# A decoder step's state-space scan: the masked step sums as two products over high and low parts

## The chip, the cores and the metric

The kernel runs on one core of one Trainium2 chip. The metric is the device time of one execution in microseconds. A core has a matrix engine (PE, with its weight loads shown apart as PEld), a vector engine (DVE), a scalar engine (ACT), a general engine (POOL) and queues for transfers, most of them issued by SP. Each engine works through its own row of instructions in order and waits on semaphores for the others.

## The reference

One inference step of a two-layer hybrid decoder for 512 prompt tokens and 32 sample tokens (8 sequences of 4) that share the weights; width 1024, all in float32.

```
even: x += 0.5*SwiGLU(rms(x))
      x += W_out[ chunk-gMLP(A) || Mamba-2 SSD(B) ](rms(x) @ W_in)
      x += 0.5*SwiGLU(rms(x))
odd:  x += 0.5*SwiGLU(rms(x))
      x += W_out[ multi-scale pool(C) || sliding-window attention(D) ](rms(x) @ W_in)
      x += 0.5*SwiGLU(rms(x))

ssd_scan (B; 16 heads of 64 in 2 groups, state 128, chunks of 128 tokens)
    xd = x * dt;  da = dt * a
    a_cum = cumsum(da over the chunk)
    seg[i, j] = a_cum[i] - a_cum[j]
    lmat  = exp(where(i >= j, seg, -inf))
    cb    = C @ B^T
    y_diag = (cb * lmat) @ xd
    ... chunk states, carried from chunk to chunk, added to y
```

The change lies in `lmat`. The difference `seg[i, j]` is the sum of the steps `da` of the tokens after j up to i, and the kernel makes it as such a sum, by a matrix product with a triangle of ones.

## The kernel before

The 544 tokens (sample first, `T` = 544, `NS` = 32) lie along the free dimension of tiles of 128 channels. Each phase (`f10`, `even`, `f20`, `f11`, `odd`, `f21`) is written as one function, and a scheduler at build time turns the written order, the priorities and the free tiles of the pools into one fixed row per engine. A change in one place can therefore shift the interleaving behind it.

Big products are float32 by parts: activations and weights are split into a high part h in `float32r` (the matrix engine's faster float32 format, `F32R` in the code) and a low part l, the rest, also in `float32r`. `mm` (L198 to L209) adds h·wh, l·wh and h·wl for 8 blocks of 128 rows in two halves of 272 columns: 48 records of L207 for one projection, into an accumulator `acc`, of which there are two. `prod` (L247) does the same for the feed-forward parts as L253. A weight's parts are made by ACT (L192) and DVE (L193) from a staging tile S.

The even mixer (`even`, L777 on) runs in this written order: the step sizes `dt` and `da` (L832); twelve conv projections with their eviction `xr` (L877), taps on DVE (L884) and activation, kept in the tiles `act`; the new conv state (L895 to L911; its tiles nco go out by POOL's transfers L902 and L911); the prompt scan; then the projections for V (L1027, L1028) and `ya`, the gate z, and `out_proj`. These later projections are what the scheduler puts between the scan's products on PE.

The scan works on 4 chunks by 2 groups, 8 steps i:

- `steps(c, g)` makes two tiles `sr` on POOL (L924): the triangle `tri_i` times da of 4 heads, 128x512 each, 16 in all. It runs two steps ahead.
- `chunk(c)` transposes the inputs into `xd`, `xdd`, `bt` and `cbm` (C·B, masked).
- `decays(g, es, cbm)` multiplies each `sr` with the triangle `tri_s` on PE (L955, a float32 product), takes exp on ACT in place (L956) and multiplies with `cbm` on DVE (L958). It runs one step ahead.
- `outputs` (L960 to L987) uses the result as the weights of the products with `xd` (L963), and brings the states on.
- `ssd_sample` (L1167 on) is a generator that advances by one part at each step i and updates the sample group's states: loads `s0`, transposes (L1250), products with `sT` (L1254), the tile `BB` on POOL (L1257), the products of `BB` (L1262), and on POOL and DVE the new states (L1264, L1265).

The pools that matter: `TT` gives tiles of the pool `big` (45 tiles of 128x544; in the even mixer they hold the 16 parts of the normed input, the 12 `act`, `rbc`, later V's and the gated half's tiles, and `BB`), `AA` gives the even mixer's 18 auxiliary tiles, `ps` four banks of accumulators for the small products. A tile is given out again when the last reader of its former content is done.

In the odd mixer the sample attention ends with the products L1693 and L1695, the eviction `sos` (L1698), a product with the matrix swap (L1701), copies into the tiles q (L1710) and their split into h and l (L262, L263), which the second half of `out_proj` reads. The small transposes L1464 and L1466 bring out the new pool state.

Of the kernel before, what the change touches and what calls it, by code (L numbers as in the profile page):

```python
# [9 lines left out]
F32 = mybir.dt.float32  # L10
F32R = mybir.dt.float32r
I32 = mybir.dt.int32
AF = mybir.ActivationFunctionType
ALU = mybir.AluOpType
# [3 lines left out]
P = 128  # L18
# [74 lines left out]
class Trunk:  # L93
# [26 lines left out]
    def TT(self, s, dt=F32):  # L120
        return self.big.tile([P, T], dt, name=self.nm(s), tag="T")
# [4 lines left out]
    def AA(self, s, dt=F32):  # L126
        return self.aux.tile([P, T], dt, name=self.nm(s), tag="A")
# [19 lines left out]
    def C(self, n):  # L147
        k, o, w = CW[n]
        return self.cst[k][:, o:o + w]
# [5 lines left out]
    @staticmethod  # L155
    def bc(ap, axis, n):
        u = ap.unsqueeze(axis)
        s = list(u.shape)
        s[axis] = n
        return u.to_broadcast(s)  # L160
# [616 lines left out]
    def even(self, nxt):  # L777
        nc, I, O, two, bc, ch, C = self.nc, self.I, self.O, self.two, self.bc, self.ch, self.C
        V, S, G, PE = nc.vector, nc.scalar, nc.gpsimd, nc.tensor
        w_in, w_out = I["ev_w_in"][0], I["ev_w_out"][0]  # L780
        xs = self.xs
        sm, RR, TT, AA, ps_ = self.small, self.RR, self.TT, self.AA, self.ps
# [48 lines left out]
        da = sm("da", [P, 5, 16])  # L831
# [8 lines left out]
        def decays():  # L840

            psd = ps_()
            dap = da[:, 0:4, :].rearrange("p c h -> p (c h)")
            PE.matmul(psd[:, 0:64], C("tri_i"), dap, start=True, stop=True)
            PE.matmul(psd[:, 64:128], C("tri_s"), dap, start=True, stop=True)
            PE.matmul(psd[:, 128:192], self.ones, dap, start=True, stop=True)
            PE.matmul(psd[:32, 192:208], C("tri_ib")[:32], da[:32, 4, :], start=True, stop=True)
            PE.matmul(psd[:, 208:224], C("tri_sb")[:32], da[:32, 4, :], start=True, stop=True)
            dax = [AA("dax"), AA("dax")]
            for g in range(2):  # L850
                V.tensor_copy(dax[g][:32, :512].rearrange("p (h q) -> p h q", h=8), bc(da[:32, 4, g * 8:g * 8 + 8], 2, 64))
            for t in range(8):
                PE.matmul(psd[:, 224 + t * 8:232 + t * 8], dax[t // 4][:32, (t % 4) * P:(t % 4 + 1) * P], C("blk_b")[:32],
                          start=True, stop=True)
            S.activation(sd[:, 0:192], psd[:, 0:192], AF.Exp)
            S.activation(sd[:32, 192:208], psd[:32, 192:208], AF.Exp)
            S.activation(sd[:, 208:288], psd[:, 208:288], AF.Exp)
# [12 lines left out]
        for u in range(6):  # L870
            un = self.unit(w_in, 0, 8, 3072 + u * 256)
            for j in range(2):
                m = u * 2 + j
                acc = self.mm(un(j), 8, xs)
                xr = RR("xr")
                with self.tc.high_priority():
                    V.tensor_tensor(two(xr), acc[:, :, :HT], two(rbc), op=ALU.mult)  # L877
                S.activation(sext[:, m, 3:7, :], xr[:, 0:NS].rearrange("p (b t) -> p t b", b=8), AF.Copy)
                S.activation(ncp[:, m, :], xr[:, T - 3:T], AF.Copy)
                a = TT("act")  # L880
                act.append(a)
                S.activation(a[:, NS:], xr[:, NS:], AF.Identity, scale=cw[:, 3, m:m + 1], bias=cb_[:, m:m + 1])
                for d in (1, 2, 3):
                    V.scalar_tensor_tensor(a[:, NS + d:], xr[:, NS:T - d], cw[:, 3 - d, m:m + 1], a[:, NS + d:],  # L884
                                           op0=ALU.mult, op1=ALU.add)
                S.activation(a[:, NS:], a[:, NS:], AF.Silu)
                if m == 5:
                    decays()
# [27 lines left out]
        scan_s = self.ssd_sample(sact, act, dt, da, ea_s, dec_s, cd_s, dsk)  # L916
        y3 = lambda ap: ap.rearrange("p (h q) -> p h q", h=8)

        def steps(c, g):

            out = []
            for h0 in (g * 8, g * 8 + 4):
                sr = AA("sr")
                G.tensor_tensor(sr[:, :512].rearrange("p (h i) -> p h i", h=4), bc(C("tri_i"), 1, 4),  # L924
                                bc(da[:, c, h0:h0 + 4], 2, P), op=ALU.mult)
                out.append(sr)
            return out

# [21 lines left out]
            return xd, bt, cbm  # L950

        def decays(g, es, cbm):
            for e in es:
                pse = ps_()
                PE.matmul(pse, C("tri_s"), e[:, :512], start=True, stop=True)  # L955
                S.activation(e[:, :512], pse, AF.Exp)  # L956
                e3 = e[:, :512].rearrange("p (h i) -> p h i", h=4)
                V.tensor_tensor(e3, e3, bc(cbm[:, g, :], 1, 4), op=ALU.mult)  # L958

        def outputs(c, g, es, xd, xdd, bt):  # L960
# [23 lines left out]
            for j in range(4):  # L984
                m = g * 4 + j
                V.scalar_tensor_tensor(act[m][:, ch(c)], act[m][:, ch(c)], dsk[:, m:m + 1], pst[:, j * P:(j + 1) * P],
                                       op0=ALU.mult, op1=ALU.add)  # L987

        es = [steps(0, 0), steps(0, 1)]
        prep = [chunk(0)]  # L990
        decays(0, es[0], prep[0][2])
        for i in range(8):
            if i + 2 < 8:
                es.append(steps((i + 2) // 2, i % 2))
            if i % 2 and i < 7:
                prep.append(chunk(i // 2 + 1))
            if i < 7:
                decays((i + 1) % 2, es[i + 1], prep[(i + 1) // 2][2])
            xd, bt, _ = prep[i // 2]
            outputs(i // 2, i % 2, es[i], *xd[i % 2], bt)  # L1000
            next(scan_s, None)
# [100 lines left out]
        for hf in range(2):  # L1102
            a = vs[hf][:NS, :512]
            V.tensor_scalar(a, a, mv[:NS, 4, 0:1], rstd[:NS, 4:5], op0=ALU.subtract, op1=ALU.mult)
            for nme, op in (("a_ln_g", ALU.mult), ("a_ln_b", ALU.add)):
                p = self.LL("lnp")
# [4 lines left out]
        for h in range(8):  # L1111
# [6 lines left out]
            t = AA("sg")  # L1118
# [678 lines left out]
```

## Time and profile before

| | us |
|---|---|
| median of 3 runs | 2309.81 (2308.47 to 2312.16) |
| the profiled execution's own time | 2307.14 |
| its span | 2305.4 |
| even mixer's conv projections and the scan | about 420 to 671 of the span |
| end of the odd mixer's attention | about 1846 to 1868 |

The mean granted clock of PE was 0.991 of full speed. The page gives busy times by engine and the chain that ended last. Groups of instructions stand by line, engine and operation, with the count, the busy time, the mean duration in ns and the idle time ahead. A matmul's record includes its pipelining, so that the durations of records in a run add up to more than the run. A float32 product of 512 columns leaves two records, a `float32r` one leaves one. In the window tables the columns are busy us of PE, PEld, DVE, ACT and POOL, each with its count, the granted clock, the share of the transfer engines and GB/s.

### The profile page before, as it was taken

To read this page: it belongs to the slowest core of one execution; us is meant where nothing else is said; L and a number is where in the kernel's file an instruction comes from. 1 tells how busy PE (TensorE), PEld (TensorE's weight loads), DVE (VectorE), ACT (ScalarE), POOL (GpSimd) and SP (SyncE) were. 2 spreads that over 40 slices of the span, in tenths; PEclk is the share of its full clock that TensorE was granted. 3 is DMA by queue.
4 is the path that set the end of the run, shared out by engine and by line. 5 is a ranking of instruction groups with operands and counts; after the bars stand their busy time and mean duration, and the time that the engine had idled before them with its cause. 6 is when DMAs were issued, how large, how long until landed. Compare 5 with 4: busy or idle time off the path is not lost.

```text
span 2305.4 us, 42876 instructions
## 1 busy us (share of the span) xinstructions
PE 2257.7 (98%) x17412; PEld 2182.9 (95%) x17412; DVE 1742.4 (76%) x2855; ACT 1069.0 (46%) x1960; POOL 610.7 (26%) x522
## 2 busy tenths in 40 slices
PE   8989999999999999999999999999999999999998
PEld 7989999998789999999999999999988899999998
DVE  7868887674459678888888888886588758778884
ACT  6434444443346354444445444444355545444442
POOL 1443330022330004333312333222032003342321
PEclk9999999999999999999999999999999999999999
DMA  4354333322422333232332233324323222323221
GB/s 147 94 115 122 91 100 111 109 77 74 124 84 91 101 106 95 90 108 83 107 107 62 83 108 90 101 93 155 101 65 101 90 77 87 108 83 108 90 85 67
DMA packets 310245, 224.21 MB, mean 97 GB/s; under 512 B 11640, under 2 KB 302864, under 8 KB 310048
## 3 DMA queue, kind: packets, MB, share of 16 engines
q1 hardware_dynamic: 303480, 203.85, 29.0%
q0 software_dynamic: 6384, 17.57, 3.1%
q8 instruction: 136, 2.23, 0.4%
q14 instruction: 61, 0.50, 0.1%
q10 hardware_dynamic: 184, 0.06, 0.0%
HBM read 203.69 MB, written 17.75 MB: 96 GB/s over the span
## 4 chain that ended last, share of the span: by engine, by line
PE 79%; issue 6%; DVE 5%; DMA 1%; ACT 1%; POOL 1%; SPq 0%; POOLq 0%; DVEq 0%; ACTq 0%
PE acc L207 39%; PE ps L253 31%; PE acc L649 1%; DVE wl L244 1%; PE ps L1254 1%; PE ps L963 1%; PE ps L1490 1%; PE ps L1534 1%; DVE wl L236 1%; PE ps L1529 0%; PE ps L955 0%; DMA S<-in_ffn_w_gu_dram 0%; DVE wl L193 0%; PE ps L1250 0%; DVE sc L1515 0%
## 5 line engine op out<-in xcount | busy, mean ns | idle before, releaser
L253 PE MATMUL ps<-h,wh 128*128 128x272 f32 x2184 | 628.0, 290 | 9.7 <-DVE g L516 6.3
L253 PE MATMUL ps<-l,wh 128*128 128x272 f32 x2184 | 629.8, 289 | 0.0
L253 PE MATMUL ps<-h,wl 128*128 128x272 f32 x2184 | 627.3, 289 | 1.9 <-DVE wl L236 1.9
L207 PE MATMUL acc<-h,wh 128*128 128x272 f32 x2768 | 592.1, 293 | 8.6 <-DVE x L689 4.8
L207 PE MATMUL acc<-l,wh 128*128 128x272 f32 x2768 | 584.4, 291 | 0.0
L207 PE MATMUL acc<-h,wl 128*128 128x272 f32 x2768 | 583.0, 291 | 0.0
L207 PEld LDWEIGHTS acc<-h,wh 128*128 128x128 f32 x2768 | 439.7, 189 | 22.8 <-issue 10.4
L207 PEld LDWEIGHTS acc<-l,wh 128*128 128x128 f32 x2768 | 438.4, 189 | 8.6 <-issue 7.9
L207 PEld LDWEIGHTS acc<-h,wl 128*128 128x128 f32 x2768 | 437.3, 189 | 6.9 <-issue 5.8
L253 PEld LDWEIGHTS ps<-h,wh 128*128 128x128 f32 x2184 | 412.3, 189 | 10.8 <-DVE g L516 7.0
L253 PEld LDWEIGHTS ps<-h,wl 128*128 128x128 f32 x2184 | 412.7, 190 | 2.1 <-DVE wl L236 2.1
L253 PEld LDWEIGHTS ps<-l,wh 128*128 128x128 f32 x2184 | 414.0, 190 | 0.0
L243 ACT ACTIVATE wh<-S 128x512 fp32r<-128x512 f32 x390 | 243.5, 629 | 291.8 <-PE ps L253 125.5
L244 DVE TENSOR_TENSOR wl<-S,wh 128x512 fp32r<-128x512 f32 x390 | 305.1, 790 | 26.7 <-ACT wh L243 25.8
L227 POOL TENSOR_TENSOR S<-S 128x512 f32<-128x512 f32 x78 | 115.1, 1476 | 546.3 <-DMA S<-in_ffn_w_gu_dram 317.4
L243 ACT ACTIVATE wh<-D 128x384 fp32r<-128x384 f32 (+1 forms) x224 | 120.6, 539 | 249.1 <-PE ps L253 185.1
L225 POOL TENSOR_TENSOR S<-S 128x512 f32<-128x512 f32 x78 | 107.5, 1378 | 470.1 <-DMA S<-in_ffn_w_gu_dram 342.7
L689 DVE SCALAR_TENSOR_TENSOR x<-acc,x 128x544 f32<-128x544 f32 x224 | 160.7, 718 | 59.2 <-PE acc L207 51.7
L244 DVE TENSOR_TENSOR wl<-D,wh 128x384 fp32r<-128x384 f32 (+1 forms) x224 | 183.2, 819 | 15.7 <-ACT wh L243 11.9
L192 ACT ACTIVATE wh<-S 128x1024 fp32r<-128x1024 f32 (+1 forms) x89 | 93.5, 1051 | 193.9 <-PE acc L207 147.1
L236 DVE TENSOR_TENSOR wl<-S,wh 128x1024 fp32r<-128x1024 f32 x98 | 155.9, 1592 | 26.1 <-ACT wh L235 24.3
L235 ACT ACTIVATE wh<-S 128x1024 fp32r<-128x1024 f32 x98 | 103.4, 1058 | 98.4 <-PE ps L253 50.2
(482 smaller groups left out, 2909.0 us busy)
## 6 DMA issues: line engine op xcount, KB each, us to landing
S<-in_ffn_w_gu_dram SPq DMA_DIRECT2D x176, 512.0 KB
D<-in_ffn_w_down_dram SPq DMA_DIRECT2D x96, 384.0 KB
S<-in_ev_w_in_dram SPq DMA_DIRECT2D x18, 1024.0 KB
S<-in_od_w_in_dram SPq DMA_DIRECT2D x10, 1024.0 KB
D<-in_ffn_w_down_dram SPq DMA_DIRECT2D x16, 512.0 KB
S<-in_ev_w_out_dram SPq DMA_DIRECT2D x8, 1024.0 KB
S<-in_od_w_out_dram SPq DMA_DIRECT2D x8, 1024.0 KB
xd<-x POOLq DMA_DIRECT2D x16, 272.0 KB, 2.4
```

What stands on the lines that cost most here:

```text
L192: nc.scalar.activation(hi[:, :nk, :n], src, AF.Copy)
L207: self.nc.tensor.matmul(acc[a][:, :HT] if type(acc) is list else acc[:, a, :HT], w[:, k, :], r[:, a * HT:(a + 1) * HT], start=k == order[0 ...
L225: G.tensor_tensor(t["S1"], u0, u1, op=ALU.add)
L227: G.tensor_tensor(t["S3"], g0, u0, op=ALU.subtract)
L235: self.nc.scalar.activation(hi, src, AF.Copy)
L236: self.nc.vector.tensor_tensor(lo, src, hi.bitcast(F32), op=ALU.subtract)
L243: self.nc.scalar.activation(hi, src, AF.Copy)
L244: self.nc.vector.tensor_tensor(lo, src, hi.bitcast(F32), op=ALU.subtract)
L253: self.nc.tensor.matmul(acc, a[:, j, :], r, start=start and j == 0 and q == 0, stop=stop and j == 3 and q == 2, skip_group_check=True)
L649: self.nc.tensor.matmul(acc[a][:, :HT], w[:, k, :], r[:, a * HT:(a + 1) * HT], start=k == 0 and i == 0, stop=k == 7 and i == 2)
L689: nc.vector.scalar_tensor_tensor(two(self.x[m]), acc[:, :, :HT], 0.5, two(self.x[m]), op0=ALU.mult, op1=ALU.add)
L963: PE.matmul(psy[:, hh * 64:hh * 64 + 64], es[hh // 4][:, (hh % 4) * P:(hh % 4 + 1) * P], xd[:, hh * 64:hh * 64 + 64], start=True, stop=True)
```

## The change

The steps are split. `dah` is da in `float32r` (ACT), `dal` the rest (DVE), and the triangle is copied into `tri_r` in the same format. `steps` then makes two tiles for each one before: `sr` from `dah` in an auxiliary tile, and `srl` from `dal` in a tile of the big pool, 32 POOL products for 16. `decays` adds two `float32r` products into the bank in the place of one float32 product, and exp writes a tile e of its own. Lines after this place are shifted: L924 is L931, L955 is L962 (high) and L963 (low), L956 is L965, L958 is L967, and what stands later moved by 9 (L1701 is L1710).

```diff
+        tri = sm("tri_r", [P, P], F32R)
+        S.activation(tri, C("tri_s"), AF.Copy)
+        dah, dal = sm("dah", [P, 4, 16], F32R), sm("dal", [P, 4, 16], F32R)
+        S.activation(dah, da[:, 0:4, :], AF.Copy)
+        V.tensor_tensor(dal, da[:, 0:4, :], dah.bitcast(F32), op=ALU.subtract)
+
         def steps(c, g):
 
             out = []
             for h0 in (g * 8, g * 8 + 4):
-                sr = AA("sr")
-                G.tensor_tensor(sr[:, :512].rearrange("p (h i) -> p h i", h=4), bc(C("tri_i"), 1, 4),
-                                bc(da[:, c, h0:h0 + 4], 2, P), op=ALU.mult)
+                sr = AA("sr", F32R), TT("srl", F32R)
+                for t, d in zip(sr, (dah, dal)):
+                    G.tensor_tensor(t[:, :512].rearrange("p (h i) -> p h i", h=4), bc(C("tri_i"), 1, 4),
+                                    bc(d[:, c, h0:h0 + 4].bitcast(F32), 2, P), op=ALU.mult)
                 out.append(sr)
             return out
...
         def decays(g, es, cbm):
-            for e in es:
+            for i, (e, l) in enumerate(es):
                 pse = ps_()
-                PE.matmul(pse, C("tri_s"), e[:, :512], start=True, stop=True)
+                PE.matmul(pse, tri, e[:, :512], start=True, stop=False)
+                PE.matmul(pse, tri, l[:, :512], start=False, stop=True)
+                e = es[i] = AA("e")
                 S.activation(e[:, :512], pse, AF.Exp)
                 e3 = e[:, :512].rearrange("p (h i) -> p h i", h=4)
                 V.tensor_tensor(e3, e3, bc(cbm[:, g, :], 1, 4), op=ALU.mult)
```

How the rows of the engines stand before and after is shown at three places. First POOL, from the last transfer of the normed input (xd) to the first of V's copies; before:

```order
L316 DMA xd_7_4900<-x_111 128x544
L902 DMA out_new_conv_prompt_dram<-nco_5864 12x3x128
L924 TENSOR_TENSOR sr_5878<-cst_even,da_5036 128x512
L924 TENSOR_TENSOR sr_5880<-cst_even,da_5036 128x512
L924 TENSOR_TENSOR sr_5882<-cst_even,da_5036 128x512
L924 TENSOR_TENSOR sr_5884<-cst_even,da_5036 128x512
L1028 COPY v_6664<-vf_6727 128x32
```

After, the same place on POOL from the thirteenth low part on (the twelve ahead of it, of the same form, follow L316's transfer):

```order
L931 TENSOR_TENSOR srl_6457<-cst_even,dal_5881 128x512
L931 TENSOR_TENSOR srl_6461<-cst_even,dal_5881 128x512
L931 TENSOR_TENSOR srl_6578<-cst_even,dal_5881 128x512
L902 DMA out_new_conv_prompt_dram<-nco_5864 12x3x128
L931 TENSOR_TENSOR srl_6582<-cst_even,dal_5881 128x512
L931 TENSOR_TENSOR sr_5884<-cst_even,dah_5880 128x512
L931 TENSOR_TENSOR sr_5888<-cst_even,dah_5880 128x512
L911 DMA out_new_conv_sample_dram<-nco_5873 4x24x128 x3
L931 TENSOR_TENSOR sr_5892<-cst_even,dah_5880 128x512
L931 TENSOR_TENSOR sr_5896<-cst_even,dah_5880 128x512
```

Fifteen of the sixteen low parts, for all four chunks, now stand ahead of L902's transfer; the high parts stay where the steps stood. Second, PE at the first decays, where `acc` is V's projection; before:

```order
L955 MATMUL ps_5924<-sr_5882,cst_even 128x512
L207 MATMUL acc_6734<-h_4859,wl_6731 128x272 x2
L207 MATMUL acc_6734<-h_4894,wh_6730 128x272
L955 MATMUL ps_5928<-sr_5884,cst_even 128x512
L207 MATMUL acc_6734<-h_4894,wh_6730 128x272
L207 MATMUL acc_6734<-l_4895,wh_6730 128x272 x2
L207 MATMUL acc_6734<-h_4894,wl_6731 128x272 x2
L1032 MATMUL acc_6786<-cst,vf_6727 128x128
L963 MATMUL ps_5932<-xd_5891,sr_5878 128x64 x4
```

After, on PE:

```order
L962 MATMUL ps_5926<-sr_5884,tri_r_5878 128x512
L963 MATMUL ps_5926<-srl_5885,tri_r_5878 128x512
L962 MATMUL ps_5932<-sr_5888,tri_r_5878 128x512
L963 MATMUL ps_5932<-srl_5889,tri_r_5878 128x512
L1041 MATMUL acc_6920<-cst,vf_6853 128x128 x4
L207 MATMUL acc_6930<-h_4673,wh_6926 128x272 x2
```

The first decays came within V's first projection, with the first outputs (L963 of before) close behind; now they come behind V's second one, in pairs, with another projection behind them. Third, PE at the end of the odd mixer's sample attention, which the diff doesn't touch; before (31 products of `acc_21908`, a group of `out_proj`, follow L1701 ahead of L1464):

```order
L207 MATMUL acc_21908<-l_21471,wh_21904 128x272 x2
L207 MATMUL acc_21908<-h_21470,wl_21905 128x272
L1701 MATMUL ps_20666<-sos_20643,cst_odd 128x512
L207 MATMUL acc_21908<-h_21470,wl_21905 128x272
L207 MATMUL acc_21908<-h_21474,wh_21904 128x272 x2
L207 MATMUL acc_21908<-l_21475,wh_21904 128x272 x2
L207 MATMUL acc_21908<-h_21474,wl_21905 128x272 x2
L207 MATMUL acc_21908<-h_21478,wh_21904 128x272 x2
```

After, on PE:

```order
L1704 MATMUL ps_20725<-spT_20678,vc_20408 128x32 x2
L1704 MATMUL ps_20725<-spT_20678,vc_20409 128x32 x2
L1710 MATMUL ps_20736<-sos_20713,cst_odd 128x512
L1473 MATMUL ps_22028<-cst,npp_20754 120x128
L1475 MATMUL ps_22028<-cst,nps_20755 128x128 x2
L207 MATMUL acc_22082<-h_22044,wh_22078 128x272 x2
L207 MATMUL acc_22144<-h_22044,wh_22140 128x272 x2
L207 MATMUL acc_22082<-l_22045,wh_22078 128x272 x2
```

The group of `out_proj` that stood around the product with swap is now ahead of it, and what follows the swap is the second half of `out_proj`, which reads the tiles that come of it.

## The prediction

> **What bounds the kernel now.** I read the page's parts 1 and 4 first, then the grouped lines, then PE's waits in the even mixer and its tables by stage. The first rows are busy times, then the chain that ended last, by engine and by line:
>
> ```profile
> span 2305.4 us, 42876 instructions
> PE 2257.7 (98%) x17412; PEld 2182.9 (95%) x17412; DVE 1742.4 (76%) x2855; ACT 1069.0 (46%) x1960; POOL 610.7 (26%) x522
> ...
> PE 79%; issue 6%; DVE 5%; DMA 1%; ACT 1%; POOL 1%; SPq 0%; POOLq 0%; DVEq 0%; ACTq 0%
> ```
>
> PE is busy for 98% of the span and carries 79% of the chain, nearly all in the products of L207 and L253. So a PE instruction taken out of its queue shortens the span by its pace, and a delay elsewhere counts only where PE has nothing else queued. The stage of the change, by grouped lines (busy us, mean ns, idle before):
>
> ```profile
> L955 PE MATMUL ps<-sr,cst_even 128*128 128x512 f32 x32 | 16.0, 592 | 0.0
> L1262 PE MATMUL ps<-BB,X 128*128 128x512 f32 x16 | 5.0, 399 | 0.0
> L956 ACT ACTIVATE sr<-ps 128x512 f32<-128x512 f32 x16 | 8.9, 598 | 2.8 <-PE ps L955 2.8
> L958 DVE TENSOR_TENSOR sr<-sr,bcm 128x512 f32<-128x512 f32 x16 | 11.3, 741 | 11.8 <-ACT sr L956 11.8
> ```
>
> Two records stand for each fp32 product of L955 (32 for 16), one for each product of L1262, which has the same size in the new format and so carries the new price. PE's waits from 410 to 865 us (us, times, longest), and tables of two stretches in the scan (window, us, PE, PEld, DVE, ACT, POOL busy, clock, DMA share, GB/s):
>
> ```profile
> PE acc L649 <- DVE g L592: 1.2, 1, 1.2
> PE ps L963 <- DVE sr L958: 0.9, 1, 0.9
> ...
> PE acc L207 <- DVE vf L1027: 0.4, 1, 0.4
> 530.00:550.00 20.00, 20.00 (x162) 17.27 (x162) 8.29 (x18) 6.59 (x11) 5.30 (x6) 1.00 0.17 53
> 650.00:670.00 20.00, 20.00 (x138) 17.40 (x138) 12.57 (x24) 6.83 (x9) 6.95 (x8) 1.00 0.48 141
> ```
>
> The scan waits once, 0.9 us, for the first decays. After that PE is full at clock 1.00 because the projections fill the places where the scan's chain (step, product, exp, multiply) would wait. The scan costs PE its own instructions and little more.
>
> **The change part by part.**
>
> *PE's products.* A record's duration includes pipelining, so I take the pace from runs of records without another between:
>
> ```profile
> 564.44 1.88 PE L955 MATMUL ps<-sr,cst_even 128*128 128x512 f32 x4
> 562.09 0.85 PE L1262 MATMUL ps<-BB,X 128*128 128x512 f32 x3
> ```
>
> Four records in 1.88 us, the last lasting 0.592: (1.88 − 0.592)/3 = 0.43 us a record, 0.86 a product. Three in 0.85, the last 0.395: (0.85 − 0.395)/2 = 0.23. The pair of new products therefore takes 0.46, and each of 16 tiles saves 0.40: −6.4 us. The lower end is no gain, if the second weight load weren't hidden and the accumulating pair ran at half pace. The upper end is −6.8, if a pair went at the 0.43 of one old record. I take −6.4, since L1262 is the same shape and kind.
>
> *The first decays* move some 9 us later in PE's row, behind V's second projection, and the first outputs behind a third. The 0.9 us wait at L963 then has its multiply done long before: −0.9 (0 to −1.3, with the 0.4 at L1027). What is late next is nothing on PE: the fillers stand ahead.
>
> *The low parts on POOL.* Sixteen more POOL products. By the changed order 15 of the low ones stand ahead of L902's transfer, for which POOL waited:
>
> ```profile
> 431.36 0.24 DVE L832 SCALAR_TENSOR_TENSOR da<-dt,aexp 128x80 f32<-128x80 f32 x1
> 495.52 0.62 POOL L902 DMA_DIRECT2D out_new_conv_prompt_dram<-nco  x1 [89.17 <-DVE nce L904]
> 496.16 6.03 POOL L924 TENSOR_TENSOR sr<-cst_even,da 128x512 f32<-128x512 f32 x4
> L924 POOL TENSOR_TENSOR sr<-cst_even,da x16: 1030/1041/2060, 496.2 to 649.9; 128x512 f32<-128x512 f32 x16
> L884 DVE SCALAR_TENSOR_TENSOR act<-xr,cols,act x36: 730/748/1527, 420.5 to 496.5; 128x511 f32<-128x511 f32 x12, 128x510 f32<-128x510 f32 x12, 128x509 f32<-128x509 f32 x12
> 435.00:457.00 22.00, 22.00 (x167) 21.88 (x166) 14.17 (x18) 11.81 (x21) 0.00 (x0) 0.92 0.30 97
> ```
>
> In the rows with three times these are the shortest, median and longest ns. POOL idles for 89 us, so its own time there costs nothing, and L902's and L911's transfers wait for no one on PE. But 15 of them at 1.04 to 1.5 us (6.03/4 beside a busy DVE) lie at about 435 to 457, among the conv taps of L884. The one tap beside POOL's products at 496 took 1527 ns against 748: +0.8. If each product costs DVE 0.8, that is 12.0 us on DVE, which has 22.0 − 14.2 = 7.8 us free there. Some 4 us must be carried as a lag; PE needs DVE only to empty an acc, of which there are two, and one group of 48 products is 6 us (0.125 each). So the lag stays inside: +0.3 (0 to +6).
>
> [...]
>
> *The rest of the scan.* The high parts take the place of the old steps, and only one low part is left in the scan, 1.04 us of POOL's 5.30 in 20. The state update has a POOL chain ahead of PE:
>
> ```profile
> 553.47 4.04 POOL L1264 TENSOR_TENSOR s<-s,sd 128x512 f32<-128x512 f32 x4 [0.46 <-PE ps L1250]
> 557.47 1.04 POOL L1257 TENSOR_TENSOR BB<-Bk,cst_even 128x512 fp32r<-128x512 f32 x1
> ```
>
> BB is done at 558.5 and used at 562.09: 3.6 us to spare. PE's scan rows get shorter and the fillers that remain are moved, about 12 us over four such updates, 3 us each, so the spare falls to 0.6: +0.5 (0 to +4, a missed L1264). Exp into a tile of its own has as many instructions as before, so nothing there; one VectorE and two ScalarE copies of 128x64 and 128x128 lie on engines with half their time free at 431: 0 (up to 0.3).
>
> *The odd mixer* isn't edited, but its PE row is interleaved anew. Before, the product with swap (L1701) had 31 filler products behind it; after, none stands between it and the first product of out_proj's second half:
>
> ```profile
> 1855.41 2.77 PE L1695 MATMUL ps<-spT,vc 128*128 128x32 f32 x12
> 1858.21 0.38 ACT L1698 ACTIVATE sos<-ps 128x256 f32<-128x256 f32 x1 [2.25 <-PE ps L1695]
> 1863.03 1.02 PE L1701 MATMUL ps<-sos,cst_odd 128*128 128x512 f32 x2
> 1864.09 1.24 DVE L1710 COPY q<-ps 64x32 f32<-64x32 f32 x8 [2.50 <-PE ps L1701]
> 1864.32 2.85 ACT L262 ACTIVATE h<-q 128x544 fp32r<-128x544 f32 x5 [3.98 <-DVE q L1710]
> 1865.26 2.61 DVE L263 TENSOR_TENSOR l<-q,h 128x544 fp32r<-128x544 f32 x4
> 1867.78 0.27 PE L1464 MATMUL ps<-cst,npp 128*120 128x128 f32 x1
> 1867.89 0.38 PE L1466 MATMUL ps<-cst,nps 128*128 128x128 f32 x2
> 1855.00:1860.00 5.00, 5.00 (x25) 4.59 (x22) 0.79 (x5) 1.55 (x4) 0.00 (x0) 0.50 0.00 0
> ```
>
> Without filler PE waits for the eviction (from 1858.18 to 1858.59: 0.41), for the copies (1864.05 to 1864.32: 0.27), for the first h (2.85/5 = 0.57), and about 0.5 for the first l behind the copies (done at 1865.9, 1.86 after the swap; four products with h fill 0.5 of it). The transposes L1464 and L1466 fill 0.25: 0.41 + 0.27 + 0.57 + 0.5 − 0.25 = +1.5 (0 to +4). The sample attention ahead of it moves too; its waits in the row before are
>
> ```profile
> PE acc L207 <- DVE kv L1354: 1.7, 1, 1.7
> PE acc L207 <- ACT h L262: 1.4, 1, 1.4
> PE acc L207 <- DVE nps L1555: 1.3, 1, 1.3
> PE ps L1534 <- ACT pT L1531: 1.1, 3, 0.7
> PE ps L1529 <- DVE sc L1515: 1.0, 1, 1.0
> ```
>
> A new interleaving may lose or gain about half of the last four, 4.8 us: 0 ± 2.4.
>
> The granted clock was 0.50 from 1855 to 1860, which doubles what PE does there. A wait in the new tail could bring one more such stretch. [...]
>
> **Sum:** −6.4 − 0.9 + 0.3 + 0.5 + 1.5 = −5.0 us. The profiled execution took 2307.14 us, 1.7 more than its span and 2.7 less than the median of 2309.8 us; on it the sum gives 2302.1, on the median 2304.8.
>
> **Rivals.** *The gain is passed on whole:* PE's 98% speaks for it, the empty tail against it. −6.4 − 0.9 = −7.3: 2302.5.
>
> *The odd mixer gives more back:* its sample attention already runs at half clock with waits, and loses 2.4 more plus the tail's upper half, 1.0: 2308.2. Against it, half of such shuffles gain.
>
> *POOL and DVE shut each other out:* the 12.0 us of DVE's delay meet the 7.8 free, but half of these lie behind a wait for PE's acc and aren't usable, so the lag is 8.1, past the 6 us of one acc by 2.1, and if that is paid at two projections with 0.8 more for one weight part, it makes 5 us: 2304.8 − 0.3 + 5 = 2309.5. For it: the 1527 ns, the 6.03 for four. Against it: in the one place where it shows, 496 to 502, PE never waited.
>
> *Slower, by the pool of big tiles:* the low parts come from the 45 tiles that also hold the 16 parts of the normed input, the 12 conv outputs and rbc: 16 + 12 + 1 + 16 = 45. V's and the gated half's evictions then need a tile that a decays product has let go. If the scan's chain runs behind the projections, PE waits for it at each of about six such places, by one exp, one multiply and a pair, 0.60 + 0.74 + 0.46 = 1.8 us: +10.8, 2315.6. For it: the count. Against it: a low part is free right after its product, before exp, and PE's row is written with the products ahead. It decides from three such waits on (2310.2), and passes the lower bound for slower at six.
>
> **How the numbers follow.** A measurement here tells 0.2%, 4.6 us, from no change: faster is under 2305.2, slower over 2314.4. Forecast as summed, 0.42, its own range 2302.5 to 2308; it is split at 2305.2 into 0.26 and 0.16. Whole gain 0.17, all faster. Odd mixer 0.16, of it 0.02 faster. POOL and DVE 0.12, of it 0.01 slower. Pool of tiles 0.13, of it 0.11 slower. Together faster 0.45, same 0.43, slower 0.12. The range begins at −6.8 − 1.3 − 2.2, 2299.5, the upper ends of the gains with a good interleaving of the odd mixer, and ends at 2311.5, the contention rival with 2 us of the odd mixer's; above lies most of the tiles' case, below next to nothing else.
>
> **What would show it.** The new products' records should be near 0.39 us and pace 0.23, some 7.4 us for 32, and PE's row of the even mixer some 7 us shorter. The wait at L963 should be gone. L884's mean should rise from 748 ns in 435 to 457 with no wait of PE there; a wait of L207 for L877 or L193 there is the contention rival. Waits of L207 for V's evictions, whose idle time ends with a decays product, are the tiles. In the tail PE should wait about 1.5 us behind the swap product. I am wrong if the new products pace at over 0.3, if PE waits anywhere in the scan by more than 3 us, or if the odd mixer's length changes by more than 4 us.

## The result, and the profile after

The changed kernel is slower, by half a per cent. Seven runs have a median of 2322.53 us (2315.02 to 2327.95), beside 2309.29 us for seven runs of the kernel before; the ratio of the two is 1.0053, 95% interval 1.0037 to 1.0069. Forecast were 2304.8 us and a range from 2299.5 to 2311.5. Two executions that took far longer than all others, 3635.83 us in e11 and 7708.13 us of the kernel before measured beside e10 and e11, are left out of every figure below. The profiled execution took 2322.53 us with a span of 2320.4, 15.0 us longer than that of before. The page's first part and the engines of the chain:

```profile
span 2320.4 us, 42922 instructions
PE 2264.4 (98%) x17412; PEld 2188.9 (94%) x17412; DVE 1753.0 (76%) x2856; ACT 1063.5 (46%) x1959; POOL 626.7 (27%) x538
...
PE 78%; DVE 6%; issue 5%; DMA 1%; ACT 1%; POOL 1%; SPq 0%; POOLq 0%; DVEq 0%; ACTq 0%
```

PE carries 6.7 us more busy time, although its instructions became cheaper: at half clock, which is shown below, the same records last longer (two of L207 0.66 us instead of 0.41). PE's waits from 410 to 880 us (us, times, longest):

```profile
PE acc L207 <- DVE vf L1036: 2.2, 2, 1.6
PE ps L962 <- DVE act L1288: 1.8, 2, 0.9
PE ps L1271 <- POOL BB L1266: 1.7, 1, 1.7
PE ps L972 <- ACT e L965: 1.4, 1, 1.4
PE acc L649 <- DVE g L592: 1.2, 1, 1.2
PE ps L810 <- DVE dtr L805: 0.8, 1, 0.8
PE ps L1271 <- DVE s L1274: 0.6, 2, 0.3
```

Where two waits of 0.9 and 0.4 us stood in the scan there are now eleven of together 8.2 us (all rows but those of L649 and L810, and two of 0.2 and 0.3 us that are not shown). V's eviction on ACT, first of before and then of after, tells what it waits for (grouped lines: busy us, mean ns, idle before and its releasers):

```profile
L1034 ACT ACTIVATE v<-acc 128x512 f32<-128x512 f32 x8 | 4.7, 586 | 0.9 <-PE acc L1032 0.9
```

```profile
L1043 ACT ACTIVATE v<-acc 128x512 f32<-128x512 f32 x8 | 4.8, 596 | 7.5 <-PE ps L963 7.3 <-PE acc L1041 0.2
L972 PE MATMUL ps<-xd,e 128*128 128x64 f32 x128 | 18.3, 306 | 1.4 <-ACT e L965 1.4
L1271 PE MATMUL ps<-BB,X 128*128 128x512 f32 x16 | 5.0, 413 | 2.3 <-POOL BB L1266 1.7 <-DVE s L1274 0.6
```

The first two rows are V's eviction into its tile v. It used to wait for V's own transposes. Now 7.3 of the 7.5 us that ACT is idle ahead of it end with L963, a low part's product: V's tiles are given out only as low parts let go of theirs. POOL's copies into the same tiles (L1037) wait 8.2 us for L963 too.

Two stretches of the scan also run at half clock. The windows are cut on the grid of 3.41 us on which all clock changes of this trace lie (us, PE with its count, PEld, DVE, ACT, POOL, clock, DMA share, GB/s):

```profile
567.55:570.96 3.41, 3.19 (x10) 0.86 (x8) 1.53 (x2) 0.65 (x1) 3.41 (x3) 1.00 0.11 17
570.96:574.38 3.42, 1.57 (x5) 0.77 (x5) 1.45 (x3) 0.00 (x0) 3.38 (x4) 0.99 0.85 290
574.38:584.62 10.24, 10.24 (x37) 8.80 (x38) 3.80 (x6) 2.06 (x4) 1.46 (x3) 0.50 0.74 207
632.37:635.79 3.42, 1.89 (x8) 0.98 (x8) 3.42 (x6) 2.32 (x3) 0.00 (x0) 1.00 0.82 239
635.79:642.61 6.82, 6.82 (x22) 4.75 (x22) 2.50 (x5) 2.54 (x4) 1.04 (x1) 0.50 1.00 301
```

In 570.96 to 574.38 PE starts five products and is busy for 1.57 us; the next 10.24 us run at 0.50. In 632.37 to 635.79 it starts eight; the next 6.82 us run at 0.50. By the granted 0.50 half of these 17.1 us, 8.5, is counted as lost; two records of L207 take 0.45 us from start to start there, 0.25 at full clock, 1.8 times as long where the prediction has the work doubled. The kernel before has no half clock in the scan.

So two quantities are kept apart below. The full-clock time of a run is its span times its mean granted clock; the rest of the span is lost to the clock. Each run lists its span and its clock, so both can be averaged over runs. (The clock is listed to three places, a step of 2.3 us here.) For the changed kernel's seven runs they are 2287.3 and 32.8 us; for the kernel before, in four sets of 17 to 23 runs, 2283.4 to 2284.4 and 21.3 to 25.2. By these seven runs the change adds 3 to 4 us at full clock and 8 to 11 us of clock; four more runs of it (e6 below) give 1 to 2 and 11 to 15.

By stage, taken in the two traces between the same evictions (us; in brackets the part at half clock that is lost):

| from, to | before | after |
|---|---|---|
| start, step sizes (L805) | 417.6 (3.4) | 419.5 (5.1) |
| conv projections, to V's first eviction | 81.7 (1.7) | 81.7 (1.7) |
| scan, V and ya, to z's first eviction | 184.2 (0) | 201.2 (8.5) |
| to out_proj's first eviction | 69.2 (0) | 62.0 (0) |
| to out_proj's last | 88.3 (0) | 91.3 (0) |
| two feed-forward parts, to the odd mixer's first eviction | 768.4 (3.4) | 768.7 (5.1) |
| odd mixer, to its last out_proj eviction | 307.1 (6.8) | 307.6 (6.8) |
| to the end | 388.9 (6.3) | 388.6 (6.0) |

The even mixer, the second to fifth of these stages, carries 12.7 of the 15.0 us: 8.5 of clock and 4.2 at full clock. These are two single traces. In a second trace of the kernel before (e9) the even mixer took 1.7 us more at full clock, a wait of L1250 in the sample states, so that the 4.2 are 2.5 beside that one; a second trace of the change (e6) agrees with the first to 0.1 us.

### The profile page after: what moved, and what is told of

Read it like the earlier page. It is cut to its first block, busy times and chain, and to the rows that moved or that the text cites. A ratio compares the mean times of both kernels' runs of the same rounds, so it can differ in the third digit from the quotient of the medians.

```text
span 2320.4 us, 42922 instructions
## 1 busy us (share of the span) xinstructions
PE 2264.4 (98%) x17412; PEld 2188.9 (94%) x17412; DVE 1753.0 (76%) x2856; ACT 1063.5 (46%) x1959; POOL 626.7 (27%) x538
## 4 chain that ended last, share of the span: by engine, by line
PE 78%; DVE 6%; issue 5%; DMA 1%; ACT 1%; POOL 1%; SPq 0%; POOLq 0%; DVEq 0%; ACTq 0%
PE acc L207 38%; PE ps L253 31%; PE acc L649 1%; DVE wl L244 1%; PE ps L1543 1%; PE ps L1538 1%; PE ps L972 1%; PE acc L682 1%; DMA D<-in_ffn_w_down_dram 1%; PE ps L1263 1%; PE ps L1499 0%; DVE wl L236 0%; DVE wl L193 0%; DMA S<-in_ffn_w_gu_dram 0%; DVE l L263 0%
## 5 line engine op out<-in xcount | busy, mean ns | idle before, releaser
L207 PE MATMUL acc<-h,wh 128*128 128x272 f32 x2768 | 592.4, 293 | 11.6 <-DVE x L689 4.8
L207 PE MATMUL acc<-l,wh 128*128 128x272 f32 x2768 | 583.3, 291 | 0.0
L207 PE MATMUL acc<-h,wl 128*128 128x272 f32 x2768 | 580.8, 290 | 0.0
L207 PEld LDWEIGHTS acc<-h,wh 128*128 128x128 f32 x2768 | 440.3, 190 | 23.9 <-issue 7.8
L207 PEld LDWEIGHTS acc<-l,wh 128*128 128x128 f32 x2768 | 438.8, 190 | 6.8 <-issue 6.0
L207 PEld LDWEIGHTS acc<-h,wl 128*128 128x128 f32 x2768 | 437.6, 189 | 4.9 <-issue 4.5
```

The source lines that it names most:

```text
L207: self.nc.tensor.matmul(acc[a][:, :HT] if type(acc) is list else acc[:, a, :HT], w[:, k, :], r[:, a * HT:(a + 1) * HT], start=k == order[0 ...
```

## The experiments

Theory T: sixteen low parts hold 16 of the 45 big tiles, V's evictions wait for them, the projections that stood between a decays product and its outputs are gone from there, PE waits, and the thin stretches bring half clock. Rival L: the lighter products alone let the clock drop. Rival P: the 16 additional POOL products delay the scan or the conv stage. All ratios are to the kernel before.

| run | median us | ratio (95%) | full clock | lost to clock |
|---|---|---|---|---|
| e1, low parts in the auxiliary pool | 2321.23 | 1.0063 (1.0047 to 1.0079) | 2285.6 | 34.0 |
| e2, before with steps in the big pool | 2326.42 | 1.0087 (1.0074 to 1.0101) | 2292.2 | 32.2 |
| e3, high parts only | 2305.68 | 0.9994 (0.9982 to 1.0007) | 2275.1 | 28.2 |
| e4, 4 low parts in the big pool | 2315.32 | 1.0026 (1.0013 to 1.0040) | 2284.4 | 27.9 |
| e5, before with idle POOL products | 2314.99 | 1.0035 (1.0023 to 1.0047) | 2286.0 | 28.1 |
| e6, the change again | 2321.05 | 1.0072 (1.0049 to 1.0096) | 2285.1 | 36.0 |
| e7, chunks 0 and 2 in the big pool | 2319.16 | 1.0036 (1.0023 to 1.0050) | 2287.6 | 28.4 |
| e8, the change, thin places filled | 2327.53 | 1.0075 (1.0057 to 1.0093) | 2299.1 | 26.8 |
| e9, before again | 2308.14 | 0.9985 (0.9970 to 1.0000) | 2283.6 | 22.8 |
| e10, 12 low parts in the big pool | 2313.07 | 1.0017 (1.0004 to 1.0031) | 2281.7 | 29.7 |
| e11, the first 8 in the big pool | 2312.57 | 1.0010 (0.9994 to 1.0026) | 2280.4 | 30.7 |

The last two columns are means over a kernel's runs; single runs scatter by 1 to 2 us at full clock and 3 to 6 us in the clock (standard deviation). That e9, the unchanged kernel, comes out at 0.9985 shows what a ratio near 1 is worth.

**e1: low parts from the auxiliary pool.**

```diff
-                sr = AA("sr", F32R), TT("srl", F32R)
+                sr = AA("sr", F32R), AA("srl", F32R)
```

> The changed kernel with the low parts in tiles of the auxiliary pool instead of the big one (16 float32r pairs as before). Theory T (the low parts hold 16 of 45 big tiles, V's evictions wait, no projection is left between a decays pair and the outputs, PE waits some 8 us in the scan and falls to half clock there): the fillers return between decays and outputs, PE's waits from 410 to 700 us fall from 9.9 to under 3 us, no stretch of half clock between 510 and 690, and the time is 2301 to 2307 us, about 5 under the kernel before. Rival L (two float32r products keep PE less busy than one float32 product, and that alone brings half clock): half clock in the scan as in the changed kernel, 2315 to 2324. Rival P (16 more POOL products in the scan are what delays it): now that more of them lie inside the scan it is slower than the change, over 2322.

Half clock all but left the scan (one stretch of 3.41 us at 516), which speaks against L: the pairs are all there. But 2321.23 us missed T's 2301 to 2307. The waits moved, from V's evictions to the first outputs, which wait for the multiply of their decays:

```profile
PE ps L972 <- DVE e L967: 5.4, 2, 3.3
```

The low parts now stood behind L902's transfer on POOL, eight products for the first four tiles, and shared 18 tiles with the exps. The even mixer was 6.3 us longer at full clock, and most of the loss to the clock lay in the odd mixer (15.4 us in this trace). P comes nearer than T here, and the run can't settle T. It also shows that a longer even mixer doesn't need the hold.

**e2: the hold alone, in the kernel before.** Float32 products, no low parts; only the pool of the 16 steps changes.

```diff
-                sr = AA("sr")
+                sr = TT("sr")
```

> The kernel before with one word changed: the 16 step tiles come from the big pool; float32 products as before, exp in place, no low parts. Theory T: the same hold without the new products, so the decays stand directly ahead of the outputs again, PE waits 5 us and more in the scan and half clock falls into it: 2315 to 2330 us, that is the change's loss plus the 6.4 us that it saves. Rival L: no half clock in the scan, 2306 to 2313. Rival P (POOL products): no change either, since their number is as before.

T's range holds: 1.0087, 8.4 us more at full clock (2292.2 against 2283.8) and 10.9 more lost to the clock, without one new product. Not all of it is the scan's: in its trace the even mixer is 6.4 us longer at full clock and the odd one, interleaved anew, 4.3; the scan loses 5.1 us to the clock. Its rows show the change's symptoms (PE's waits, two windows, V's eviction):

```profile
PE ps L1262 <- POOL BB L1257: 2.6, 1, 2.6
...
531.02:534.43 3.41, 2.43 (x15) 1.08 (x13) 2.93 (x6) 1.99 (x3) 0.00 (x0) 1.00 0.37 129
534.43:544.67 10.24, 8.84 (x49) 7.43 (x50) 3.33 (x8) 1.93 (x5) 2.04 (x2) 0.50 0.01 2
L1034 ACT ACTIVATE v<-acc 128x512 f32<-128x512 f32 x8 | 4.8, 596 | 2.1 <-PE ps L963 2.0
```

Here a step's tile is let go by L963, the outputs' product, and V's eviction waits for that. One of this trace's other waits, 1.3 us at L1250, is for a transfer and is not T's.

**e3: the high parts only** (the low parts of the steps are neither made nor used).

```diff
-                sr = AA("sr", F32R), TT("srl", F32R)
+                sr = (AA("sr", F32R),)
...
-                PE.matmul(pse, tri, e[:, :512], start=True, stop=False)
-                PE.matmul(pse, tri, l[:, :512], start=False, stop=True)
+                PE.matmul(pse, tri, e[:, :512], start=True, stop=True)
```

> The changed kernel without the low parts: one float32r product of the high part for each tile, the low part of the steps is left out. Theory T: no hold, fillers in place, PE's work in the scan 10 us less than before (0.86 to 0.23 for each of 16): 2297 to 2304 us. Rival L: the still lighter products bring more half clock, 2312 and over. Rival P: like T.

No half clock in the scan, and the even mixer 7.7 us shorter at full clock: most of the 10.1 us by the prices of the prediction. The total didn't move, and T's 2297 to 2304 us was missed: 8.7 us less at full clock, 6.9 more lost to the clock. In this trace the odd mixer, whose row of PE is interleaved anew, lost 15.4 us to the clock, beside 6.8 and 13.7 in the two traces of the kernel before. L falls: the lightest products have no half clock where they stand.

**e4, e7, e10, e11: how many low parts the big pool holds.** One condition decides which pool a low part comes from:

```diff
-                sr = AA("sr", F32R), TT("srl", F32R)
+                sr = AA("sr", F32R), (AA if c else TT)("srl", F32R)            # e4: 4 held
+                sr = AA("sr", F32R), (AA if c in (1, 3) else TT)("srl", F32R)  # e7: 8
+                sr = AA("sr", F32R), (AA if c == 3 else TT)("srl", F32R)       # e10: 12
+                sr = AA("sr", F32R), (AA if c > 1 else TT)("srl", F32R)        # e11: 8
```

> The changed kernel with only the first chunk's four low parts in the big pool and the other twelve in the auxiliary pool, so that 4 and not 16 big tiles are held and POOL makes these four ahead of L902. In the row of PE fillers stand between nearly all decays and outputs, and the pairs are 16 as in the change. Theory T (hold of the tiles: waits and thin stretches of PE in the scan): the waits of PE from 495 to 690 us under 3 us, no half clock there, the even mixer from V's first eviction to out_proj's last 5 to 7 us shorter than before at full clock; what the time is then hangs on the odd mixer, whose row is interleaved anew here too: 2296 to 2312 us. Rival L (the pair of products is what lets the clock drop): half clock in the scan again and 2315 or more. Rival P (the 16 POOL products inside the scan): waits of PE behind POOL as in the run with all low parts in the auxiliary pool, 2315 or more.

> The changed kernel with the low parts of chunks 1 and 3 in the auxiliary pool and those of chunks 0 and 2 in the big pool: 8 of 45 big tiles held instead of 16. All decays have fillers behind them again in the row of PE, and the odd mixer's row is near that of before (nine tenths of its products in the same order). Theory T: the even mixer 4 to 6 us shorter than before at full clock, no half clock between 510 and 690, time 2300 to 2309 beside a kernel before of 2305 to 2309. Rival L (the float32r pairs bring half clock by themselves): half clock in the scan, 2313 and more. Rival P (the POOL products): PE waits behind POOL, evictions or weight parts in the conv stage, 2312 and more.

> The changed kernel with the last chunk's four low parts in the auxiliary pool and the other twelve in the big pool: four big tiles stay free for V's evictions, and the row of PE has fillers behind all decays of the middle of the scan. The two runs with four and eight low parts in the big pool saved 5 to 6 us of PE's work and lost 4 to 7 of it again to waits that the auxiliary pool brought (exp tiles at L972, splits and gates in front of out_proj). Theory T': the tie of V's evictions needs all 16 held, so PE's waits from 515 to 690 fall under 3 us and no half clock is in the scan, and with only four tiles more in the auxiliary pool the waits of 700 to 765 stay under 3 us: even mixer 2 to 5 us shorter than before at full clock, 2303 to 2312 us. Rival (any hold brings the thin scan): half clock between 510 and 690 again, 2316 and more.

> The changed kernel with the low parts of the first two chunks in the big pool and those of the last two in the auxiliary one; its row of PE in the odd mixer is close to that of the change (the tail without filler behind the swap product). Theory T': as for twelve in the big pool in the scan (no half clock there, waits under 3 us), with waits of 2 to 5 us in front of out_proj from the eight tiles in the auxiliary pool: even mixer 0 to 4 us shorter than before at full clock, 2304 to 2316 us. Rival: half clock in the scan again, 2316 and more.

With four tiles or more left to V the thin scan is gone: e4, e10 and e11 have no half clock there, e7 one stretch of 3.4 us at 516. In e10 the 16 pairs remain, and PE's waits from 410 to 850 us and the groups are:

```profile
PE acc L207 <- DVE l L263: 2.4, 2, 1.5
PE ps L810 <- DVE dtr L805: 0.8, 1, 0.8
PE acc L207 <- DVE vf L1036: 0.7, 2, 0.5
PE ps L977 <- ACT e L965: 0.5, 1, 0.5
...
L972 PE MATMUL ps<-xd,e 128*128 128x64 f32 x128 | 15.2, 271 | 0.0
L962 PE MATMUL ps<-sr,tri_r 128*128 128x512 f32 x16 | 6.4, 400 | 0.0
L963 PE MATMUL ps<-srl,tri_r 128*128 128x512 f32 x16 | 6.3, 393 | 0.0
L1043 ACT ACTIVATE v<-acc 128x512 f32<-128x512 f32 x8 | 4.7, 585 | 0.4 <-PE acc L1041 0.4
```

V's eviction waits 0.4 us again, PE's waits in the scan are 1.2 us (L207 for L1036 and L977), and there is no half clock from 457 to 876. The even mixer is 3.0 us shorter than before at full clock, 2.8 in e11. Against the change e10 and e11 are some 9 us faster for one condition on a pool.

They don't beat the kernel before, 1.0017 and 1.0010. The remaining gap isn't in the even mixer: both lose 5 to 6 us more to the clock than the kernel before in the same set (29.7 and 30.7 against 24.7 us). Where they lose it, the traces don't settle: the odd mixer lost 13.7 us in e10's and 18.8 in e11's, beside 6.8 and 13.7 in the two of the kernel before. E10 missed T's time of 2303 to 2312 by 1 us, e11 met its own. E4 and e7, with 4 and 8 low parts in the big pool, also had no thin scan, but little or no saving. In e7 PE waits, from 410 to 850 us:

```profile
PE acc L207 <- DVE l L263: 2.4, 2, 1.4
PE ps L972 <- DVE e L967: 2.0, 1, 2.0
PE acc L207 <- DVE wl L193: 1.8, 1, 1.8
PE ps L1126 <- DVE vs L1117: 1.1, 1, 1.1
```

T's numbers for e4 and e7 (5 to 7 and 4 to 6 us shorter at full clock) were too good: the even mixer was 1.0 us shorter and 1.5 us longer. Their times, 2315.32 and 2319.16 us, lie where the rivals L and P had put theirs, though L's half clock is missing. The wait at L972 and those at the splits and gates of the mixer's end, whose tiles come from the auxiliary pool, suggest that the low parts there are in the way; that isn't shown. E10 waits as long for the splits (l L263, 2.4 us), and e11, with as many low parts in the auxiliary pool as e7, kept its saving. So the number held doesn't put these four runs in order; what they share is that with 12 or fewer held the thin scan is gone.

**e5: the POOL products alone, in the kernel before.** PE's row is the same as before.

```diff
+        jk = TT("jk")
+        for q in range(15):
+            G.tensor_tensor(jk[:, :512].rearrange("p (h i) -> p h i", h=4), bc(C("tri_i"), 1, 4),
+                            bc(da[:, q // 4, (q % 4) * 4:(q % 4) * 4 + 4], 2, P), op=ALU.mult)
         sd = sm("sd", [P, 288])
```

> The kernel before with 15 POOL products of the low parts' size and place added (into one tile that nobody reads), between L316's and L902's transfers; the row of PE is the same word for word. Theory T and the prediction's step: POOL 22 us busy from 435 to 457, DVE's two-input instructions there longer by 4 to 5 us in all, PE without a wait: within 1 us of the kernel before. Rival P: evictions or weight parts late, 2308 to 2312 beside a kernel before of 2305.7 (+3 to +6).

Here T's reading was wrong, and the prediction's rival of POOL and DVE was right that this stage can be made to wait: +0.35%, some 8 us. POOL began straight behind da, at 430.67, six microseconds earlier than in the changed kernel; four taps of L884 (L888 in this kernel) took 5.92 us (a tap's median was 0.75 us before), and one low weight part came late (PE's waits, then POOL and DVE in order of time: start, us):

```profile
PE acc L207 <- DVE wl L193: 1.8, 1, 1.8
...
430.67 24.11 POOL L835 TENSOR_TENSOR jk<-cst_even,da 128x512 f32<-128x512 f32 x15 [23.23 <-DVE da L832]
438.22 5.92 DVE L888 SCALAR_TENSOR_TENSOR act<-xr,cols,act 128x509 f32<-128x509 f32 x4
```

In this trace the conv stage grew by 3.5 us, 1.8 at full clock and 1.7 of clock. That is part of the 8 us; the mean loss to the clock rose by 5.6, of which this stage explains 1.7, and where the rest lies is open. The changed kernel doesn't pay this: its conv stage took 81.7 us as before.

**e6: the change again.**

> The changed kernel once more, for a second trace of it beside the others on the same chip. Theory T: the thin stretches of PE around 571 to 574 and 632 to 636 us, where the decays pair, the outputs and the products of BB stand without a projection between them, bring half clock again in at least one of the two places; full-clock time of the even mixer 3 to 5 us over before. If the half clock of the first trace was chance, none is in the scan here. 2316 to 2326 us.

```profile
570.16:573.57 3.41, 1.46 (x4) 0.67 (x4) 1.25 (x3) 0.00 (x0) 3.41 (x4) 1.00 0.91 300
573.57:583.81 10.24, 10.14 (x37) 8.72 (x37) 3.91 (x7) 2.06 (x4) 1.62 (x4) 0.50 0.73 207
631.60:635.01 3.41, 1.87 (x8) 0.92 (x7) 3.41 (x6) 2.25 (x3) 0.00 (x0) 1.00 0.82 234
635.01:641.84 6.83, 6.83 (x22) 4.76 (x21) 2.45 (x5) 2.60 (x4) 1.04 (x1) 0.50 1.01 300
```

Both half-clock stretches come back at the same products, with the same waits, in both traces of the change and in neither of the kernel before. They belong to the row, not to chance.

**e8: the change with idle products in the thin places.**

```diff
                 V.tensor_tensor(e3, e3, bc(cbm[:, g, :], 1, 4), op=ALU.mult)
+            if len(prep) > 1:
+                psd = ps_()
+                for _ in range(8):
+                    PE.matmul(psd, tri, l[:, :512], start=True, stop=True)
```

> The changed kernel with eight products more behind each of the last six decays steps (float32r, 128x512, into a bank that nobody reads): 48 x 0.23 = 11.0 us of idle work for PE at the thin places of the scan, all else as in the change; the odd mixer's row is that of the kernel before. Theory T (thin stretches of PE bring half clock there): no half clock between 560 and 650, part of the waits of PE filled, so that the 11 us of work cost 3 us or less against the change: 2316 to 2325 us. If half clock came from something else than PE's idle and thin places (DVE, transfers, the format), it stays and the work is added: 2328 to 2335.

```profile
568.29:571.70 3.41, 1.75 (x8) 0.90 (x7) 0.25 (x1) 0.00 (x0) 3.41 (x4) 1.00 0.70 223
571.70:575.11 3.41, 3.15 (x8) 2.12 (x8) 2.23 (x4) 1.06 (x3) 1.36 (x3) 0.50 0.82 250
575.11:585.35 10.24, 10.24 (x70) 8.97 (x69) 3.27 (x5) 1.11 (x3) 1.25 (x2) 1.00 0.54 152
631.44:642.00 10.56, 9.14 (x52) 7.09 (x53) 6.66 (x10) 4.97 (x6) 1.40 (x2) 1.00 0.91 273
```

Of 17.1 us at half clock 3.4 remain with the 48 products, which speaks for the thin stretches as the cause. The loss to the clock fell from 32.8 and 36.0 to 26.8 us. The waits stayed (BB still 1.7 us late), so that the 11.0 us of work lay on the path in full: 2327.53 us, 5 over the change and 2.5 over T's upper end, where the 3 us that T allowed for the work was too little.

**e9: the kernel before again.**

> The kernel before once more, for a second trace. Theory T's last part (the 3.41 us grid of the clock stands differently to the program in each execution): same row, same full-clock time within 2 us, but other thin places of the odd mixer hit: half clock stretches that differ from those of the first trace by some 3 to 10 us in place or length. 2303 to 2313.

The odd mixer shows the grid at two places of one row. The same products of one row (16 of 128x2, then the scores) in the first trace of before, and then in this one:

```profile
1651.00:1654.42 3.42, 3.42 (x31) 3.42 (x30) 1.95 (x2) 3.42 (x6) 0.85 (x2) 1.00 0.25 86
1654.42:1657.83 3.41, 3.41 (x26) 2.58 (x26) 2.18 (x13) 0.56 (x1) 0.00 (x0) 1.00 0.71 230
1657.83:1668.07 10.24, 10.24 (x79) 9.70 (x78) 9.31 (x32) 5.37 (x21) 0.00 (x0) 1.00 0.08 27
```

```profile
1653.70:1657.11 3.41, 3.41 (x31) 3.06 (x29) 1.89 (x5) 2.43 (x4) 0.00 (x0) 0.99 0.15 32
1657.11:1667.35 10.24, 10.24 (x38) 8.25 (x38) 7.90 (x33) 2.96 (x14) 0.00 (x0) 0.50 0.27 93
```

In the first, the edge at 1654.42 divides the small products (they start at 1653.30) and the clock stays. In the second they start at 1654.46 and lie with the scores in one window, and 10.24 us at half clock follow. The odd mixer of this one kernel lost 6.8 us in one execution and 13.7 in the other. So a single trace can't tell which kernel's odd mixer loses more.

## Why the prediction was wrong

*PE's products: right, a little large.* The new products run as forecast: 0.23 us from one start to the next in the first pairs of the change's trace (515.15 to 515.84), with L963's own weight loads of 189 ns hidden beside them, and records of 400 and 393 ns in e10. From start to start, decays and projections together took 332.0 us (8.5 and 323.5, at full clock and without waits) from the step sizes to out_proj's last eviction before and 327.1 in e10 (7.5 and 319.6), 4.9 less (6.2 in e7), against 6.4. Counted the same way, the changed kernel itself spends about 4.4 less: the saving was there, and PE's waits outgrew it.

*The first decays: wrong.* The wait at L963 went, as forecast, but "the fillers stand ahead" was read from one side only. Behind the next four decays none stands any more: in the trace's row, from 553.9 to 635.4 us, no product of L207 lies between the pairs of a step and its outputs, where 7, 18, 8 and 20 lay before. The row of e2 has none at these four places either, that of e10 has 7, 19, 8 and 17. And V's evictions, 2.2 us of waiting for L207, were late next.

*POOL in the conv stage: right in the sum, mis-sized inside.* POOL ran the 15 products early:

```profile
436.78 21.98 POOL L931 TENSOR_TENSOR srl<-cst_even,dal 128x512 fp32r<-128x512 f32 x15 [28.73 <-DVE dal L923]
435.00:457.00 22.00, 22.00 (x172) 21.88 (x171) 18.57 (x19) 8.03 (x19) 20.22 (x15) 0.95 0.15 49
```

DVE grew from 14.17 to 18.57 us there, +4.4 and not 12.0, and PE had no wait. E5 shows that a start 6 us earlier is enough to make one.

*The scan's POOL chain: the term was too small.* 0.5 was put down, with 4 as its end; BB and the states cost 2.3 us (1.7 and 0.6).

*The odd mixer:* +1.5 was forecast; between the two traces it is 0.5 us, with the same loss to the clock, and 1.4 at full clock between the second traces, e6 and e9. Behind the emptied tail PE waits 0.47 us for sos and 0.34 for the first h.

*The pool of big tiles: this is the step that failed.* The sum has no term for it; PE's waits in the scan rose from 1.3 to 8.2 us. The rival had the mechanism and a price of 10.8 us; the even mixer lost 4.2 at full clock where 6.4 should have been gained, which makes 10.6. That the two are so near is luck: the price was six waits of 1.8 us behind V's evictions, and only two such waits stand in the trace, 2.2 us together. The other 6 us are waits of the scan and of the sample states (L962, L972, L977, L1271, L942), nearly all at places where no product of L207 stands just ahead in the row. The rival was given 0.13, on the ground that a low part is free right after its product and that "PE's row is written with the products ahead". The row is written that way because the scheduler found V's projections blocked (e2 brings the same about by the hold alone, and e10, with four tiles free, undoes it): the tie had already been paid for in the row, as pairs and outputs without filler, and that could be read from it.

*The clock: not in the sum at all.* The scan lost 8.5 us to it, more than half of the 15.0 us that the change's trace is longer. The prediction names half clock only in the odd tail, as one more stretch that a wait could bring, and has no term for it. In the changed kernel the longest gap ahead of a half-clock stretch in the scan is 1.66 us (the wait for BB). In the traces of before and after the stretches, but for the last at each run's end, are 3.41, 6.83 or 10.24 us long, and e9 shows the grid displaced against the same row: the edge of a window lay 1.12 us behind the start of the 16 small products in the first trace of before, 0.76 us ahead of it in e9. What else decides after which window half clock comes isn't shown.

Open remains why kernels with another row in the odd mixer (e3, e10, e11) lose 5 to 7 us more to the clock on average; that thin places fall differently on the grid is possible, not shown. E5, whose row of PE is that of before, loses 5.6 more too.

## What to carry to other kernels

Where a scheduler orders the engines, a new tile costs the work that can no longer get one: count what a pool must hold at once, and read in the new row what stands behind each dependent product, not only ahead of it. Here the saving on a full PE was kept where the filler stayed, the independent work that the scheduler puts between dependent products (e10, even mixer 3.0 us shorter at full clock), and lost where it went (the change, 4.2 us longer). Compare span times clock as well as span, over several runs: in e3 a row that was 8.7 us cheaper at full clock lost 6.9 of it to the clock.

## What the hardware showed

Half clock came without a gap of PE over 1.66 us ahead of it in the changed kernel's scan: a 3.41 us window with five products and 1.57 us of busy PE was followed by 10.24 us at 0.50, and more products in such places (e8) left 3.4 of 17.1 us at half clock. In e9 a window of 31 records with PE busy throughout, 16 of them 128x2, was followed by 10.24 us at 0.50 as well. The first trace of the same kernel kept its clock there, with the window's edge inside the 16; its odd mixer lost 6.8 us in one trace and 13.7 in the other. With these losses apart, the full-clock times of one kernel's runs scattered by 1 to 2 us, the times themselves by 3 to 5.
